# Two rounds of token rows dispatched at once, in float32r products of a high and a low part

## The chip, the cores and the metric

The kernel runs on one core of a Trainium2 chip. Its time is device microseconds of one execution. The core's engines run side by side, each with its own stream of instructions: TensorE (PE) for products, VectorE (DVE), ScalarE (ACT), GpSimd (POOL) and SyncE (SP), which here issues the transfers. Weights come from HBM; tiles lie in SBUF (128 partitions), products go to PSUM.

## The reference

256 tokens of width 1024 pass through a block with a mixer, a cross attention and an expert layer, and then through further stages of the same kind; the kernel meets three expert layers in all. An expert layer computes, for 16 experts in 4 groups:

```
gidx  = best of 4 groups;  eidx = best 2 of the 4 experts in it;  ew = softmax(2 values) * gval
combine[t, e] = weight of expert e for token t, 0 for the 14 others
for e in 16 experts:
    he = silu(t @ w_gate[e]) * (t @ w_up[e])
    y += combine[:, e] * (he @ w_down[e])
```

Each token uses two experts, so the kernel brings tokens to the experts that want them instead of computing all pairs. `w_gate` and `w_up` are 1024x512, `w_down` 512x1024, in float32.

## The kernel before

An expert layer is the function `moe`. First comes the routing: ACT and DVE normalise the rows of the tokens into `xs` (two tiles of 128 tokens x 1024), the logits are formed, and a chain of small DVE operations and an exponential on ACT (L941) picks the experts; products with a triangular matrix (L1053) count each token's place among those of its expert, and `pm` (L1055) holds it. `places` (L1184) then builds one-hots `O`: for two rounds at a time, O[token, slot] is 1 where the token stands in that slot. A round is 128 slots, cut among two to four experts by `ROUNDS`; there are seven rounds (p = 0 to 6).

For each round TensorE does in order:

- `pg` and `pu`: the gate and the up product of the round's 128 slots (`times`, `prod`, L1078), over eight row blocks of the weights.
- `pP`: transposes of the round's one-hots (`back`, L1098), used later to bring results back.
- `px`: the *dispatch* of the next round (L1066): the rows of the tokens are brought to the slots as 8 blocks of xs^T O, each summed over two token tiles. In float32 each product of 128x128 is two instructions, so that a dispatch is 32 of them, in two halves of 16. DVE multiplies the result by the column scale into `XT` (L1068), POOL adds the shift where there is one (L1070).
- `hid`: DVE multiplies silu(pg) by pu (L1090), then `ph` transposes it on TensorE (L1092), and ACT copies it back (L1093). The first half of the next dispatch stands ahead of ph, the second half behind.
- `py`: the down product (L1078 again), then `pc` (L1128, L1129) adds the weighted results to the tokens' rows `x`.

The weight of each slot comes from `slot_weights`, every second round: products `pw` of the one-hots with the experts' weights (L1212), and small DVE reductions `ws` (L1217). The first round's dispatch is `first_inputs` (L1197), evacuated by ACT (L1199, L1201).

The weights are streamed by `Stream.load` (L125) in units of 1 MiB in the fixed order of a plan, into a ring of 20 units; a unit's slot is refilled when its products are done. A tile scheduler sets the order of the instructions on each engine from the order of the code and the buffers; instructions inside `pin` keep their order in the program. `warm` issues filling products on TensorE. After round 3, `extras` is a branch for experts that have more tokens than slots; it isn't entered here.

Of the kernel before, what the change touches and what calls it, by code (L numbers as in the profile page):

```python
# [44 lines left out]
NP8, NP4, NP2 = 22, 2, 7  # L46
# [165 lines left out]
class Kernel:  # L212
# [774 lines left out]
    def moe(self, sx, sc_v, sh_v, first, x, units, ahead=None, start=None, hook=None, st=None, tail=0):  # L987
# [41 lines left out]
        xs = self.b8("xs")  # L1029
        if first:  # L1030
            pin(nc.scalar.activation(xs[:, D:], x[:, D:], AF.Copy, scale=rs[:, 1:2]))
            pin(nc.vector.tensor_scalar(xs[:, :D], x[:, :D], rs[:, 0:1], None, ALU.mult))
        else:
            pin(nc.scalar.activation(xs[:, D:], x[:, D:], AF.Identity, bias=off[:, 1], scale=rs[:, 1:2]))
            pin(nc.vector.tensor_scalar(xs[:, :D], x[:, :D], mu[:, 0], rs[:, 0:1], ALU.subtract, ALU.mult))
# [12 lines left out]
        S.moes += 1  # L1048
        pp = self.aux("pos")
# [10 lines left out]
        def dispatch(O, xt):  # L1060

            for k0 in range(0, 8, 4):
                ps = self.aux("px")
                for c in range(4):
                    for t in range(2):
                        nc.tensor.matmul(ps[:, c * P : (c + 1) * P], xs[:, t * D + (k0 + c) * P : t * D + (k0 + c + 1) * P], O[:, t * P : (t + 1) * P].bitcast(F32), start=(t == 0), stop=(t == 1))  # L1066
                xo = xt[:, k0 : k0 + 4, :]
                nc.vector.tensor_mul(xo, ps[:].rearrange("p (c s) -> p c s", c=4), sc_v[:, k0 : k0 + 4].unsqueeze(2).to_broadcast([P, 4, P]))  # L1068
                if sh_v is not None:
                    nc.gpsimd.tensor_add(xo, xo, sh_v[:, k0 : k0 + 4].unsqueeze(2).to_broadcast([P, 4, P]))  # L1070
                yield
# [8 lines left out]
        def times(xt, get, ps, r):  # L1080
            for kh in range(2):
                ws = get()
                for c in range(4):
                    k = kh * 4 + c
                    prod(ps[:], xt[:, k, :], ws, c, k == 0, k == 7, r)
                del ws
# [84 lines left out]

        def places(p, pm):


            O, out, n0 = self.b2("O", F32R), [], slots(p)[0][0]
            for r in range(p, min(p + 2, len(ROUNDS))):
                o = O[:, (r - p) * 256 : (r - p) * 256 + 256]
                out.append(o)
                o = o.rearrange("p (t s) -> p t s", t=2)
                for w in sorted(set(ROUNDS[r])):  # L1180
                    same = [(s - n0, c) for s, c in slots(r) if CAPS[s] == w]
                    s0, c0, n = *same[0], len(same)
                    sh = [P, 2, n, w]
                    nc.vector.tensor_tensor(  # L1184
                        o[:, :, c0 : c0 + n * w].rearrange("p t (e s) -> p t e s", e=n),
                        pm[:, :, s0 : s0 + n].unsqueeze(3).to_broadcast(sh),
                        self.cst(C_IOTA, w).unsqueeze(1).unsqueeze(1).to_broadcast(sh), ALU.is_equal)
            return out

        def first_inputs(O):  # L1190
            xt = self.b4("XT", F32, (P, 8, P))
            for k in range(8):
                if k % 2 == 0:
                    ps = (self.mm if k > 2 else self.aux)("px")
                q = ps[:, k % 2 * P : k % 2 * P + P]
                for t in range(2):
                    nc.tensor.matmul(q, xs[:, t * D + k * P : t * D + (k + 1) * P], O[:, t * P : (t + 1) * P].bitcast(F32), start=(t == 0), stop=(t == 1))  # L1197
                if sh_v is None:
                    nc.scalar.activation(xt[:, k, :], q, AF.Copy, scale=sc_v[:, k : k + 1])  # L1199
                else:  # L1200
                    nc.scalar.activation(xt[:, k, :], q, AF.Identity, bias=sh_v[:, k : k + 1], scale=sc_v[:, k : k + 1])  # L1201
            return xt

        def inputs(O):
            xt = self.b4("XT", F32, (P, 8, P))
            return xt, dispatch(O, xt)
# [16 lines left out]
        xt = first_inputs(Os[0])  # L1223
# [69 lines left out]
        def prepare(px, pw):  # L1293
# [5 lines left out]
            for k in range(8):  # L1299
                q = px[:, k * 32 : (k + 1) * 32]  # L1300
                for t in range(2):
                    ww = slice(t * D + k * P, t * D + (k + 1) * P)
                    nc.tensor.matmul(q, xs[:, ww], O[:, t, 0, :].bitcast(F32), start=(t == 0), stop=(t == 1))
# [89 lines left out]
        for p in range(LAST + 1):  # L1393
            n = len(ROUNDS[p])
            get, downs = (lambda: [S.raw() for _ in range(n)]), (lambda: [S.raw(down=True) for _ in range(n)])
            if p % 2 == 0:
                wsl = slot_weights(p, Os)
            PT = Os.pop(0)
# [9 lines left out]
            if p == 0 and start is not None:  # L1408
                start(xs)
# [3 lines left out]
            del xt  # L1413
            back(PT, self.aux("pP"))
            if p % 2 and p < LAST:
                s0 = slots(p + 1)[0][0]
                Os = places(p + 1, pm[:, :, s0:])
            if p < LAST:
                xt, fill = inputs(Os[0])
                next(fill)  # L1420
# [3 lines left out]
            if p == LAST:  # L1424
                del xs
# [646 lines left out]
```

## Time and profile before

| | us |
|---|---|
| median of 3 runs | 1337.19 (1334.74 to 1338.62) |
| the profiled execution | 1337.22 |
| its span | 1335.5 |
| TensorE busy | 1248.1 (93%) |
| DVE busy | 714.1 (53%) |
| ACT busy | 405.2 (30%) |
| POOL busy | 127.9 (10%) |
| mean granted TensorE clock | 0.974 of full speed |

The busy shares are averages over stages of different kinds. The expert layers are where transfers run near 420 GB/s for 200 us at a time and DVE is busy for only two or three tenths; between them DVE and ACT are busier and the transfers slower. What a change in one stage is worth is to be read from that stage's own timeline.

### The profile page before, as it was taken

Reading aid. Unit: us, or ns where it says so; the run is one execution under the profiler, and the core shown is the slowest. Engines: PE = TensorE matmul, PEld = TensorE weight load, DVE = VectorE, ACT = ScalarE, POOL = GpSimd, SP = SyncE. Lnnn points to the kernel's source line nnn. Section 1 sums busy time; section 2 is a strip of 40 time slices with the busy share of each in tenths; the row PEclk is TensorE's granted clock in tenths of the full one; section 3 lists DMA queues with packets and bytes.
Section 4 is the critical chain, followed back from the end, with each engine's and each line's share of the span. In section 5 each row is a group of like instructions: output and inputs, shape, how many; then the busy total and the mean of one; then the engine's idle time right before and its main releaser. Section 6 shows DMA issues by size and latency. Waiting matters only on the chain. (4 is left out here: it accounts for less than half of the span.)

```text
span 1335.5 us, 18792 instructions
## 1 busy us (share of the span) xinstructions
PE 1248.1 (93%) x7149; PEld 786.4 (59%) x7149; DVE 714.1 (53%) x1422; ACT 405.2 (30%) x687; POOL 127.9 (10%) x136
## 2 busy tenths in 40 slices
PE   6999988999979989999999979989999999997995
PEld 5677867744334459977543334388988874433442
DVE  5797996532212149875732212388999754222224
ACT  4576434310000034654311000243345541000011
POOL 1000200000000020232010001031102000001001
PEclk9899998899999999999999989999999999998998
DMA  9857795779999997688599999977788578999990
GB/s 375 324 189 266 276 373 225 281 306 421 421 418 422 418 420 273 225 317 314 195 394 421 421 417 421 419 297 267 270 313 318 189 315 323 423 420 419 420 390 31
DMA packets 64509, 445.75 MB, mean 334 GB/s; under 512 B 7380, under 2 KB 7892, under 8 KB 12048
## 3 DMA queue, kind: packets, MB, share of 16 engines
q1 hardware_dynamic: 62352, 439.91, 82.9%
q10 hardware_dynamic: 1440, 3.13, 0.6%
q8 instruction: 61, 1.00, 0.3%
q0 software_dynamic: 608, 1.32, 0.3%
q14 instruction: 48, 0.39, 0.1%
HBM read 443.28 MB, written 1.05 MB: 333 GB/s over the span
## 5 line engine op out<-in xcount | busy, mean ns | idle before, releaser
L173 DVE TENSOR_TENSOR hl<-w,hl 128x1024 fp32r<-128x1024 f32 (+1 forms) x154 | 190.9, 1249 | 51.2 <-ACT hl L172 50.9
L172 ACT CAST hl<-w 128x1024 fp32r<-128x1024 f32 (+1 forms) x160 | 164.9, 1040 | 175.8 <-PE dn L426 107.4
L1078 PE MATMUL pg<-w,XT 128*64 128x512 f32 (+1 forms) x864 | 179.1, 613 | 0.0
L1078 PE MATMUL pu<-w,XT 128*64 128x512 f32 (+1 forms) x864 | 162.2, 593 | 0.0
L1078 PE MATMUL py<-w,hid 128*64 128x512 f32 (+2 forms) x912 | 155.7, 573 | 2.0 <-ACT hid L1093 2.0
L812 DVE SCALAR_TENSOR_TENSOR acc<-w,sc,acc 128x512 f32<-128x512 f32 x168 | 130.2, 779 | 1.6
L1090 DVE TENSOR_TENSOR hid<-hid,pu 128x512 f32<-128x512 f32 x21 | 14.4, 687 | 207.2 <-PE pu L1078 195.7
L1078 PEld LDWEIGHTS pu<-w,XT 128*64 128x64 f32 (+1 forms) x864 | 49.9, 125 | 95.6 <-issue 92.9
L1078 PEld LDWEIGHTS pg<-w,XT 128*64 128x64 f32 (+1 forms) x864 | 49.0, 128 | 96.8 <-issue 94.1
L1078 PEld LDWEIGHTS py<-w,hid 128*64 128x64 f32 (+1 forms) x912 | 48.8, 125 | 90.7 <-issue 81.2
L1401 ACT ACTIVATE hid<-pg 128x512 f32<-128x512 f32 x21 | 12.5, 597 | 209.8 <-PE pg L1078 209.8
L1131 DVE TENSOR_TENSOR x<-x,pc 128x512 f32<-128x512 f32 (+1 forms) x90 | 54.9, 647 | 32.8 <-PE pc L1129 32.2
L1066 PE MATMUL px<-O,xs 128*128 128x128 f32 x576 | 70.8, 276 | 0.0
L1066 PEld LDWEIGHTS px<-O,xs 128*128 128x128 f32 x576 | 67.2, 192 | 3.4 <-issue 3.4
L1117 DVE SCALAR_TENSOR_TENSOR y<-py,ws,gate 128x512 f32<-128x512 f32 x26 | 19.5, 751 | 66.0 <-PE py L1078 66.0
L1070 POOL TENSOR_TENSOR XT<-XT,adaT 128x512 f32<-128x512 f32 x24 | 25.0, 1042 | 299.0 <-DVE XT L1068 289.2
L424 PE MATMUL dn<-hl,h 128*128 128x512 f32 (+1 forms) x128 | 50.8, 403 | 2.9 <-ACT hl L172 2.9
L1118 ACT CAST yh<-y 128x512 fp32r<-128x512 f32 x26 | 16.1, 619 | 120.8 <-DVE y L1117 120.8
L425 PE MATMUL dn<-hl,h 128*128 128x512 f32 (+1 forms) x128 | 51.3, 401 | 0.8 <-DVE hl L173 0.8
L424 PE MATMUL dn<-hl,e 128*128 128x512 f32 x128 | 51.2, 400 | 0.0
L426 PE MATMUL dn<-hl,h 128*128 128x512 f32 (+1 forms) x128 | 51.0, 398 | 0.0
L426 PE MATMUL dn<-hl,e 128*128 128x512 f32 x128 | 49.9, 390 | 0.0
(547 smaller groups left out, 2261.1 us busy)
## 6 DMA issues: line engine op xcount, KB each, us to landing
w<-e SPq DMA_DIRECT2D x282, 1024.0 KB, 14.3
w<-w SPq DMA_DIRECT2D x78, 1024.0 KB, 7.6
w<-wa SPq DMA_DIRECT2D x48, 1024.0 KB, 6.8
w<-e SPq DMA_DIRECT2D x12, 512.0 KB, 16.8
xT<-xT SPq DMA_DIRECT2D x2, 512.0 KB, 5.1
w<-w SPq DMA_DIRECT2D x4, 256.0 KB, 7.0
x<-x SPq DMA_DIRECT2D x2, 512.0 KB, 11.3
mem<-mem SPq DMA_DIRECT2D x2, 512.0 KB, 3.9
```

The source lines that it names most:

```text
L172: a = k.nc.scalar.copy(hi, w)
L173: b = eng.tensor_sub(lo, w, hi.bitcast(F32))
L424: nc.tensor.matmul(o, a, wh[:, c, :], start=(first and c == 0), stop=False)
L425: nc.tensor.matmul(o, a, wl[:, c, :], start=False, stop=False)
L426: nc.tensor.matmul(o, b, wh[:, c, :], start=False, stop=(last and c == m - 1))
L812: pin(nc.vector.scalar_tensor_tensor(acc[:], w[:, j, :], c, acc[:], ALU.mult, ALU.add))
L1066: nc.tensor.matmul(ps[:, c * P : (c + 1) * P], xs[:, t * D + (k0 + c) * P : t * D + (k0 + c + 1) * P], O[:, t * P : (t + 1) * P].bitcast(F ...
L1070: nc.gpsimd.tensor_add(xo, xo, sh_v[:, k0 : k0 + 4].unsqueeze(2).to_broadcast([P, 4, P]))
L1078: nc.tensor.matmul(out[a : a + w, :], lhs[:, a : a + w], ws[e][(slice(None), c, *h)], start=start, stop=stop, tile_position=(0, a))
L1117: nc.vector.scalar_tensor_tensor(y, py, w, gate[:, n * 512 : n * 512 + 512], ALU.mult, ALU.mult)
L1118: nc.scalar.copy(yh, y)
L1131: nc.vector.tensor_add(a, a, pc)
```

## The change

The normalised rows are kept as two float32r tiles instead of one float32 tile: `xh`, the rows rounded by a cast on ACT, and `xl`, the rest, a subtraction on DVE (`low`). In the second and third expert layers the rows are normalised in place in `x` first. A dispatch then serves the two rounds whose one-hots lie in one tile: for each of 8 blocks, four float32r products (xh and xl, two token tiles) with a moving operand of 256 columns, which are the two rounds' one-hots. It runs at the start (for rounds 0 and 1) and in rounds 1, 3 and 5 (for 2 and 3, 4 and 5, and for 6 alone, with the operand repeated). Results of 128x256 are scaled and shifted in one instruction, by ACT and DVE in turn; `first_inputs` and POOL's additions are gone. `slot_weights` is moved behind the up product. Two pools of tiles are larger by one, and the scratch for DMA descriptors is set to 4096.

```
-NP8, NP4, NP2 = 22, 2, 7
+NP8, NP4, NP2 = 23, 3, 7
...
-        xs = self.b8("xs")
+        xh, xl = self.b8("xh", F32R), self.b8("xl", F32R)
         if first:
-            pin(nc.scalar.activation(xs[:, D:], x[:, D:], AF.Copy, scale=rs[:, 1:2]))
-            pin(nc.vector.tensor_scalar(xs[:, :D], x[:, :D], rs[:, 0:1], None, ALU.mult))
+            for t in range(2):
+                pin(nc.scalar.activation(xh[:, t * D : (t + 1) * D], x[:, t * D : (t + 1) * D], AF.Copy, scale=rs[:, t : t + 1]))
         else:
-            pin(nc.scalar.activation(xs[:, D:], x[:, D:], AF.Identity, bias=off[:, 1], scale=rs[:, 1:2]))
-            pin(nc.vector.tensor_scalar(xs[:, :D], x[:, :D], mu[:, 0], rs[:, 0:1], ALU.subtract, ALU.mult))
+            pin(nc.scalar.activation(x[:, D:], x[:, D:], AF.Identity, bias=off[:, 1], scale=rs[:, 1:2]))
+            pin(nc.vector.tensor_scalar(x[:, :D], x[:, :D], mu[:, 0], rs[:, 0:1], ALU.subtract, ALU.mult))
+            for t in range(2):
+                pin(nc.scalar.copy(xh[:, t * D : (t + 1) * D], x[:, t * D : (t + 1) * D]))
+
+        def low(t, lo, hi):
+            c = slice(t * D + lo, t * D + hi)
+            if first:
+                pin(nc.vector.scalar_tensor_tensor(xl[:, c], x[:, c], rs[:, t : t + 1], xh[:, c].bitcast(F32), ALU.mult, ALU.subtract))
+            else:
+                pin(nc.vector.tensor_sub(xl[:, c], x[:, c], xh[:, c].bitcast(F32)))
...
         S.moes += 1
+        low(0, 0, D)
+        low(1, 0, 512)
...
-        def dispatch(O, xt):
+        def dispatch(Os, xt):
...
+            O = [o.rearrange("p (t s) -> p t s", t=2) for o in Os]
+            for k in range(8):
+                if k % 2 == 0:
+                    ps = self.aux("px")
+                q = ps[:, k % 2 * 256 : k % 2 * 256 + 256]
+                for t in range(2):
+                    ww = slice(t * D + k * P, t * D + (k + 1) * P)
+                    o = both[:, :, t, :] if len(Os) == 2 else O[0][:, t].unsqueeze(1).to_broadcast([P, 2, P])
+                    for i, part in enumerate((xh, xl)):
+                        nc.tensor.matmul(q, part[:, ww], o, start=(t == i == 0), stop=(t == i == 1))
+                y = xt[k // 4][:, k % 4, :]
+                if k % 2:
+                    nc.vector.tensor_scalar(y, q, sc_v[:, k : k + 1], 0.0 if sh_v is None else sh_v[:, k : k + 1], ALU.mult, ALU.add)
+                elif sh_v is None:
+                    nc.scalar.activation(y, q, AF.Copy, scale=sc_v[:, k : k + 1])
+                else:
+                    nc.scalar.activation(y, q, AF.Identity, bias=sh_v[:, k : k + 1], scale=sc_v[:, k : k + 1])
+                if k % 4 == 3:
+                    yield
...
         Os = places(0, pm0[:, :, 0::4])
         self.warm(WARM_INPUTS[S.moes - 1])
-        xt = first_inputs(Os[0])
+        low(1, 512, D)
+        xt, fill = inputs(Os)
+        self.do(fill)
...
-            if p % 2 == 0:
-                wsl = slot_weights(p, Os)
-            PT = Os.pop(0)
...
             times(xt, get, pu, p)
-            del xt
+            if p % 2 == 0:
+                wsl = slot_weights(p, Os)
+            PT = Os.pop(0)
             back(PT, self.aux("pP"))
+            fill = ()
             if p % 2 and p < LAST:
+                del xt
                 s0 = slots(p + 1)[0][0]
                 Os = places(p + 1, pm[:, :, s0:])
-            if p < LAST:
-                xt, fill = inputs(Os[0])
+                xt, fill = inputs(Os)
                 next(fill)
             hidden(hid, pu, self.aux("ph"))
             self.do(fill)
...
-    nc = bacc.Bacc("TRN2", target_bir_lowering=False, num_devices=1)
+    nc = bacc.Bacc("TRN2", target_bir_lowering=False, num_devices=1, dynamic_dma_scratch_size=4096)
```

Three places show how the instructions move. The first is TensorE at the end of round 0 of the first expert layer, from the last up product to the first down product; before:

```order
L1078 MATMUL pu_2350<-w_250_1797,XT_2231 64x512
L1098 MATMUL pP_2441<-cst,O_2223 128x128 x2
L1066 MATMUL px_2446<-O_2223,xs_2160 128x128 x8
L1092 MATMUL ph_2456<-cst,hid_2351 128x128 x4
L1066 MATMUL px_2463<-O_2223,xs_2160 128x128 x8
L1078 MATMUL py_2473<-w_265_1892,hid_2351 64x512
```

And after, from the same up product:

```order
L1101 MATMUL pu_2361<-w_250_1797,XT_2236 64x512
L1225 MATMUL pw_2453<-cbr_2343,O_2226 128x32 x4
L1121 MATMUL pP_2462<-cst,O_2226 128x128 x2
L1115 MATMUL ph_2466<-cst,hid_2362 128x128 x4
L1101 MATMUL py_2473<-w_265_1892,hid_2362 64x512
```

The products px on both sides of the transposes ph are gone from this round, and the products pw have come to stand behind the up product.

The second is ACT in the routing of the second expert layer; `pr` is the exponential, `gate` a row of the residual gate. Before:

```order
L1025 COPY lpart_6983<-lp_6973 128x256
L1034 ACTIVATE xs_6987<-x_78,off_6968,xn_6941 128x1024
L941 ACTIVATE pr_7016<-pr_7016 128x32
L901 ACTIVATE gate_6993<-gate_6994,cst 128x512
L901 ACTIVATE gate_6993<-gate_7004,cst 128x512
```

And after:

```order
L1026 COPY lpart_7208<-lp_7198 128x256
L1035 ACTIVATE x_78<-x_78,off_7193,xn_7166 128x1024
L1038 CAST xh_7212<-x_78 128x1024 x2
L902 ACTIVATE gate_7221<-gate_7222,cst 128x512
L942 ACTIVATE pr_7244<-pr_7244 128x32
L902 ACTIVATE gate_7221<-gate_7232,cst 128x512
```

Two casts are added ahead of the exponential, and one gate row that stood behind it now stands ahead of it.

The third is DVE in round 0 of the second expert layer, at the hidden product (`hid`); `kk` and `tab` belong to a table for the block that follows. Before:

```order
L1686 TENSOR_SCALAR tab_7239<-tab_7239 128x256
L1678 TENSOR_SCALAR kk_7240<-kk_7240 128x256
L1090 TENSOR_TENSOR hid_7188<-hid_7188,pu_7187 128x512
L1679 TENSOR_SCALAR kk_7240<-kk_7240 128x256
L1682 SCALAR_TENSOR_TENSOR tab_7239<-kk_7240,ang_7236 128x256
```

And after:

```order
L1694 TENSOR_SCALAR kk_7478<-kk_7478 128x256
L1230 TENSOR_REDUCE ws_7562<-pw_7563 64x1
L1695 TENSOR_SCALAR kk_7478<-kk_7478 128x256
L1230 TENSOR_REDUCE ws_7562<-pw_7563 64x1
L1698 SCALAR_TENSOR_TENSOR tab_7477<-kk_7478,ang_7474 128x256
L1230 TENSOR_REDUCE ws_7562<-pw_7563 64x1
L1698 SCALAR_TENSOR_TENSOR tab_7477<-kk_7478,tab_7477 128x256
L1230 TENSOR_REDUCE ws_7562<-pw_7563 64x1
L1698 SCALAR_TENSOR_TENSOR tab_7477<-kk_7478,tab_7477 128x256
L1113 TENSOR_TENSOR hid_7426<-hid_7426,pu_7425 128x512
```

The reductions of pw, which were done long before, now stand ahead of the hidden product, with operations of the table between them.

## Rows read from the trace of the kernel before

**Rows 1.** Windows, first layer: us, busy PE, PEld, DVE, ACT, POOL; PEclk; DMA; GB/s.
```profile
401.00:484.00 83.00, 81.84 (x403) 34.33 (x404) 16.19 (x30) 11.45 (x18) 0.57 (x1) 0.98 1.01 420
```
**Rows 2.** Timeline of TensorE, end of round 0: start, us, engine, line, operation.
```profile
285.21 0.44 PE L1098 MATMUL pP<-cst,O 128*128 128x128 f32 x2
285.48 1.95 PE L1066 MATMUL px<-O,xs 128*128 128x128 f32 x16
287.27 0.60 PE L1092 MATMUL ph<-cst,hid 128*128 128x128 f32 x4
287.71 1.95 PE L1066 MATMUL px<-O,xs 128*128 128x128 f32 x16
289.59 0.65 PE L1078 MATMUL py<-w,hid 128*64 128x512 f32 x2
```
**Rows 3.** Timeline of TensorE, end of round 6 of the first layer.
```profile
474.20 0.44 PE L1098 MATMUL pP<-cst,O 128*128 128x128 f32 x2
475.12 0.66 PE L1092 MATMUL ph<-cst,hid 128*128 128x128 f32 x4 [0.48 <-DVE hid L1090]
476.45 1.08 PE L1078 MATMUL py<-w,hid 128*64 128x512 f32 x4 [0.68 <-ACT hid L1093]
```
**Rows 4.** Timeline of TensorE, slot weights of the third layer's round 0.
```profile
1106.63 0.62 PE L1212 MATMUL pw<-cbr,O 128*128 128x32 f32 x4
```
**Rows 5.** Timeline of TensorE, a run of 128x256 products behind the first layer.
```profile
498.19 0.28 PE L442 MATMUL dt<-b,hl 128*128 128x256 f32 x1
...
499.99 0.28 PE L442 MATMUL dt<-b,hl 128*128 128x256 f32 x1
```
**Rows 6.** Timeline of TensorE, start of the first layer's dispatch and products.
```profile
265.69 3.36 PE L1197 MATMUL px<-O,xs 128*128 128x128 f32 x28
...
270.63 1.94 PE L1078 MATMUL pg<-w,XT 128*64 128x512 f32 x8
```
**Rows 7.** Timeline of all engines, routing and start of the second layer.
```profile
637.13 1.24 ACT L1034 ACTIVATE xs<-x,off,xn 128x1024 f32<-128x1024 f32 x1
...
639.51 0.23 ACT L941 ACTIVATE pr<-pr 128x32 f32<-128x32 f32 x1 [1.14 <-DVE pr L940]
...
639.82 0.69 ACT L901 ACTIVATE gate<-gate,cst 128x512 f32<-128x512 f32 x1
...
642.28 0.26 DVE L928 SCALAR_TENSOR_TENSOR sl<-er,go 128x16 fp32r<-128x16 f32 x2
...
643.65 0.17 DVE L1055 SCALAR_TENSOR_TENSOR pm<-pos,sl 128x32 f32<-128x32 f32 x1
...
644.43 3.06 PE L1197 MATMUL px<-O,xs 128*128 128x128 f32 x24 [0.22 <-DVE O L1184]
...
649.51 2.79 PE L1078 MATMUL pg<-w,XT 128*64 128x512 f32 x12
```
**Rows 8.** Lines by form, casts and subtractions: count, busy us, mean ns, idle before.
```profile
L173 DVE TENSOR_TENSOR hl<-w,hl 128x1024 fp32r<-128x1024 f32 x150 | 188.2, 1264 | 50.7 <-ACT hl L172 50.4
L172 ACT CAST hl<-w 128x1024 fp32r<-128x1024 f32 x156 | 162.4, 1051 | 175.0 <-PE dn L426 107.4 <-PE dt L443 43.9 <-PE cv L426 11.8
```
**Rows 9.** Lines, the reductions of the slot weights.
```profile
L1217 DVE TENSOR_REDUCE ws<-pw 64x1 f32<-64x2 f32 (+2 forms) x48 | 7.5, 157 | 17.8 <-PE pw L1212 17.2
```
**Rows 10.** Timeline of DVE, the table's operation in the second layer's round 0.
```profile
667.86 0.42 DVE L1682 SCALAR_TENSOR_TENSOR tab<-kk,ang 128x256 f32<-128x256 f32 x1
```
**Rows 11.** Source view of line 125, the unit issued at 335.9 us.
```profile
DMA to landing us min/median/max: 16.9/16.9/16.9
```
**Rows 12.** Timeline of TensorE, first product of round 3.
```profile
357.55 0.59 PE L1078 MATMUL pg<-w,XT 128*32 128x512 f32 x1
```
**Rows 13.** Lines, weight loads of the dispatch.
```profile
L1066 PEld LDWEIGHTS px<-O,xs 128*128 128x128 f32 x576 | 67.2, 192 | 3.4 <-issue 3.4
```
**Rows 14.** Timeline of TensorE, its first products behind the first layer.
```profile
492.47 2.84 PE L355 MATMUL b<-cst,x 128*128 128x128 f32 x16 [3.06 <-DVE x L331]
```
**Rows 15.** Windows of TensorE: us, busy, granted clock, DMA share, GB/s.
```profile
494.00:496.00 2.00, 2.00 (x12) 0.50 1.04 434
```

More of the change, by code (lines that the diff above doesn't have):

```diff
@@ L1058, in moe @@
         del pp
-        def dispatch(O, xt):
[L1062 to L1071, printed above, removed]
+        def dispatch(Os, xt):
[18 more added lines that the diff above has]
+                    yield
         def prod(out, lhs, ws, c, start, stop, r, *h):
@@ L1084, in times @@
                     k = kh * 4 + c
-                    prod(ps[:], xt[:, k, :], ws, c, k == 0, k == 7, r)
+                    prod(ps[:], xt[kh][:, c, r % 2 * P : r % 2 * P + P], ws, c, k == 0, k == 7, r)
                 del ws
@@ L1170, in tiles @@
             }
+        both = None
         def places(p, pm):
+            nonlocal both
             O, out, n0 = self.b2("O", F32R), [], slots(p)[0][0]
+            both = O[:].rearrange("p (r t s) -> p r t s", r=2, t=2)
             for r in range(p, min(p + 2, len(ROUNDS))):
@@ L1188, in places, with inputs @@
             return out
[L1190 to L1206, printed above, removed]
+        def inputs(Os):
+            xt = [self.b4("XT", F32, (P, 4, 256)) for _ in range(2)]
+            return xt, dispatch(Os, xt)
         def slot_weights(p, Os):
@@ L1302, in prepare @@
                     ww = slice(t * D + k * P, t * D + (k + 1) * P)
-                    nc.tensor.matmul(q, xs[:, ww], O[:, t, 0, :].bitcast(F32), start=(t == 0), stop=(t == 1))
+                    for i, part in enumerate((xh, xl)):
+                        nc.tensor.matmul(q, part[:, ww], O[:, t, 0, :], start=(t == i == 0), stop=(t == i == 1))
             nc.vector.tensor_mul(xt, px[:, :256].rearrange("p (c s) -> p c s", c=8), sc_v.unsqueeze(2).to_broadcast([P, 8, 32]))
@@ L1408, in moe @@
             if p == 0 and start is not None:
-                start(xs)
+                start(x)
             if p == XP - 1:
@@ L1424, in moe @@
             if p == LAST:
-                del xs
+                del xh, xl, xt
             down(hid, downs, wsl[:, p % 2 : p % 2 + 1], PT, tiles(p == LAST), p, p == LAST)
```

## The prediction

> **What bounds the kernel now.** I read the page's 40 slices first, then the stretches by engine, then TensorE's timeline over the ends of single rounds, then all engines over the starts of the expert stages, and last when weights were issued, landed and were used. The profiled execution took 1337.22 us, 1335.5 of it span; the median of the runs is 1337.19, so the sum below is made against 1337.2 and needs no shift.
>
> Inside an expert stage the reader is to see two limits close together. TensorE is busy 81.84 of the 83 us from 401 to 484, at a granted clock of 0.98, while the DMA engines are busy all the time (share 1.01, 420 GB/s) [rows 1]. So TensorE's instructions, and the waits between them, set the end, as long as weights keep ahead.
>
> At the end of a round with a dispatch, TensorE goes from the transposes pP through 16 products, the four transposes ph, 16 products more, to py: 285.21 to 289.59, 4.38 us. Sixteen of these products fill 1.79 us (285.48 to 287.27), and they also fill the wait for the hidden product (DVE) and its copy (ACT) [rows 2]. In the last round, which dispatches nothing, those two waits stand open (0.48 and 0.68 us) and pP to py takes 474.20 to 476.45, 2.25 us [rows 3]. This pair is the heart of the forecast: a dispatch taken out is worth 4.38 - 2.25 = 2.13 us, not the 3.58 that its products take.
>
> **A round without a dispatch.** In rounds 0, 2 and 4 the dispatch is gone: -2.13 each. The products pw (0.62 us, [rows 4]) move from the middle of the pg products to behind the pu products in rounds 0 and 4, into the wait for the hidden product. There they cost about nothing, since they and the transposes pP (0.27 until the next start, rows 2) together last about as long as pP and the open 0.48 of rows 3: -0.6 more. Rounds 0 and 4 give -2.7 each. In round 2 pw stays inside a run of products; half of its dispatch lies among the pu products, where it fills no wait, so that nearly its full 1.79 goes; behind ph the other half gives way to an open wait, 2.32 us from ph to py in rows 2 against 1.33 in rows 3, -1.0. That is -2.8 at most; I take -2.6. Round 6 had no dispatch and gains only its pw, which is half as long: -0.3.
>
> **A round with a dispatch for two.** Rounds 1, 3 and 5 now have 32 float32r products of 128x256. The nearest rows are the dt products, float32r with 256 columns and a new weight for each: from 498.19 to 499.99 there are 15, 0.12 us each [rows 5]. So 32 take 3.84 us. With pP (0.27) and ph (0.44 from 287.27 to the next start) the way to py is 4.55 us against 4.38: +0.2 each. The bounds of the price: below, the two float32 instructions' own pitch of 1.79/16 = 0.112 (32 of these are 3.58, then +0.0); above, twice 0.12, if the moving operand, which here is two runs of 128 columns that begin 256 columns apart, and not one run of 256, streams at half the pace. I take 0.12, the row with the same count of columns and the same type. In the last dispatch the second run repeats the first; I price it alike. The evacuations change engine (eight of 128x256, half on ACT and half on DVE, for two DVE products and two Pool additions); both engines are idle there, and TensorE writes two of them in 0.96 us. I cost them at nothing but the tail behind the last product, which is hidden in the down products.
>
> Rounds together: -2.7 - 2.6 - 2.7 - 0.3 + 3 x 0.2 = -7.7 us per stage, three times.
>
> **The start of the first expert stage.** Products start at 265.69 and the gate products are in an unbroken run from 270.63 on, two of them (0.44) having come earlier: they stand as if begun at 270.2 [rows 6]. Now all 32 products stand ahead of pg. The low parts (about 0.8 us per 1024, and 1.5 us of them before the one-hots) lie mostly under the wait for the positions' products; I let the dispatch start 0.6 later, at 266.3. 266.3 + 3.84 + 0.35 for the last evacuation = 270.5: +0.3. If none of the low parts were covered it would be +1.9.
>
> **The start of the other two.** Here something is added to the chain that decides. In [rows 7] ACT normalises the second token tile (637.13, 1.24 us), then waits, then does the routing's exponential at 639.51, which waited for DVE. In the changed order two casts of 1024 columns, 1.05 us each [rows 8], and one gate row (0.69) stand ahead of that exponential: 638.37 + 2.10 + 0.69 = 641.16, so it comes 1.65 later. All of DVE's routing is queued behind that exponential, and behind it the positions, the one-hots and the first product. Then the low parts, 1.26 and about 0.69 (half of the subtraction in rows 8 and a fixed part), stand ahead of the one-hots' positions pm. But seven small operations of the routing that stood there now come later: sl at 642.28 to pm at 643.65 was 1.37 and becomes 0.36 + 1.95 = 2.31. First product: 644.43 + 1.65 + 0.94 = 647.0. Pg then stands as if begun at 647.0 + 3.84 + 0.35 = 651.2, against 649.51 - 0.44 = 649.07: +2.1 with rounding down for what overlaps. The bounds: +0.5 if the scheduler's order lets the casts hide under the wait of 1.14 that ended with the exponential, +4 if TensorE's clock falls in its longer wait (below). I take +2.0 for each of the two stages.
>
> **The second stage's round 0.** There DVE also builds a table for the block that follows (tab, 0.42 each, [rows 10]), and before the hidden product it has a wait for pw now: four small reductions of pw (0.16 each, [rows 9]) alternate with table operations, and the hidden product is behind them all. pw can start only when pu has ended. So the hidden product starts at 0.62 + 4 x 0.16 + 3 x 0.42 + 0.2 = 2.7 us after pu's end, instead of at once; TensorE waits: +2.7, which swallows this round's gain. If the pw reductions were through earlier it is 0; if a further table operation slips ahead, +3.2. The first and third stages have the hidden product ahead of the reductions: nothing.
>
> **The limit by weights.** In the first stage the smallest lead that I found is at the start of round 3: a unit issued at 335.9 landed 16.9 us later, at 352.8 [rows 11], and its products started at 357.55 [rows 12]: 4.7 us ahead. The sum asks -2.7 + 0.2 - 2.6 + 0.3 = -4.8 by then. I take 0.4 off the first stage's gain. The third and second stage ask 3.1 and 0.4 by that place, less than this lead; if it were fully gone, each us asked beyond it would be lost.
>
> **Sum.** First stage -7.7 + 0.3 + 0.4 = -7.0; second -7.7 + 2.0 + 2.7 = -3.0; third -7.7 + 2.0 = -5.7. Together -15.7: 1337.2 - 15.7 = 1321.5, and I forecast 1321.
>
> The larger pools and the smaller scratch for DMA descriptors I cost at nothing: the ring's length and the order of the loads stay. Pool loses 24 additions in a time in which nothing waited for it but the next round's input.
>
> **Weight loads, a rule against the change.** Each dt product of rows 5 has its own load of a 128x128 weight, and the dispatch's loads took 192 ns [rows 13]; yet the products follow at 0.12. Loads lie beside products in flight. The Trainium skill, page "TensorE: Matmul & The Clock Gate", Part 3, "What overlaps and what doesn't", says that a weight load overlaps products in flight only where row groups differ; here all are full height. By that rule a dispatch would be 32 x (0.12 + 0.19) = 9.9 us, 6.1 more for each of 12, and the time 1395. The trace's 0.12 and 0.112 contradict it, so it has no chance of its own beyond a part of the third rival's.
>
> **Rivals.**
> 1. TensorE's clock. After a wait of 3.06 us on TensorE [rows 14] the stretch 494 to 496 had a granted clock of 0.50, 1.2 GHz [rows 15]. In the second and third stage TensorE's wait ahead of the first product grows from 0.22 (rows 7) to 2.8, and in the second stage's round 0 by 2.7. If the dispatch behind that wait runs at half the clock it takes 3.84 us more, twice: 1329. For it: the wait is nearly as long as in rows 14. Against it: filling products (the calls of warm) stand just ahead of it. The same page, "HAM oscillation — how this bites in real kernels", says that pauses between bursts send the next burst to the half clock; rows 14 and 15 agree, and by it the time would be this rival's.
> 2. Weights bind for longer than I allow: the DMA share of 1.01 says that nothing can be fetched faster, and each us that TensorE gains shortens the lead. If only half of the rounds' gain survives in all stages (-23.1 / 2 instead of -23.1), the time is 1333. For it: rows 1. Against it: in rows 1 TensorE, not the wait for weights, filled the stretch.
> 3. Slower: the moving operand in two runs streams at half pace. 32 products then take 7.68 us, +3.84 for each of 12 dispatches: +46, 1368. The sum turns at a price of 0.12 + 15.7 / 384 = 0.161 us per product. For it: no row of before shows a moving operand in two runs in float32r. Against it: in no row that I read does an operand's layout change the pace; rows 2 pass 128 columns at a time at nearly the pace of rows 5.
> 4. The even rounds' waits grow more than rows 3 show, or DVE's and ACT's evacuations hold up the hidden product in the odd rounds; with 0.7 us in each of 18 rounds the gain is 3 us: 1334.
> 5. Better: the low parts and casts are covered, and the second stage's round 0 keeps its gain: 1321.5 - 2 x 1.5 - 2.7 = 1316, and to 1313 if the odd rounds cost nothing and the start is shorter.
>
> **Chances.** The forecast, within 4 us of 1321: 0.54. Clock: 0.13. Weights: 0.10. Growing waits: 0.08. Better: 0.08. Half pace or some other price above 0.16: 0.07. What a measurement of this kernel tells from no change is about 0.3%, 4 us. Faster by more than that: forecast, clock, better, and most of weights and of growing waits: 0.84. Within it: 0.07. Slower: 0.09, with half pace and a start that is worse than every bound. The range leaves out the half pace and the best of the better: 1312 to 1335; the forecast's own is 1317 to 1326.
>
> **What would show it.** In the changed profile the two-round products follow each other at 0.12 us; pP to py takes about 2.3 us in even rounds (5 in round 0 of the second stage) and 4.5 in odd ones. The routing's exponential is 1.7 us later behind the casts, the first product of the second stage comes 2.6 later, and its granted clock stays at 1.00. Py of the first stage's round 2 or pg of round 3 waits a little for a DMA. A pitch above 0.16, a clock of 0.5 at the starts, or waits for weights in rounds 4 to 6 would make the prediction wrong.

## The result, and the profile after

The changed kernel takes 1345.36 us (1344.72 to 1348.17) against 1337.63 for the kernel before on the same chip: a ratio of 1.0065, 95% interval 1.0044 to 1.0087. It is slower by 8 us where 16 us of gain were forecast. The profiled execution has a span of 1343.1 us. TensorE does less than before (1248.1 us busy before), and the end comes later all the same:

```profile
span 1343.1 us, 18206 instructions
PE 1238.3 (92%) x6861; PEld 758.4 (56%) x6861; DVE 714.7 (53%) x1442; ACT 422.8 (31%) x716; POOL 102.5 (8%) x112
```

The first place to look at is a round with a dispatch. This is TensorE's timeline at the end of round 1 of the first layer, in the columns of [rows 2]:

```profile
310.02 0.44 PE L1121 MATMUL pP<-cst,O 128*128 128x128 f32 x2
...
310.41 0.28 PE L1085 MATMUL px<-O,xl 128*128 128x256 f32 x1
310.53 0.28 PE L1085 MATMUL px<-O,xh 128*128 128x256 f32 x1
310.65 0.28 PE L1085 MATMUL px<-O,xl 128*128 128x256 f32 x1
...
311.24 0.28 PE L1115 MATMUL ph<-cst,hid 128*128 128x128 f32 x1
311.55 0.39 PE L1085 MATMUL px<-O,xh 128*128 128x256 f32 x1
...
312.61 0.49 PE L1115 MATMUL ph<-cst,hid 128*128 128x128 f32 x3
312.85 0.36 PE L1085 MATMUL px<-O,xh 128*128 128x256 f32 x1
...
313.98 1.07 PE L1101 MATMUL py<-w,hid 128*64 128x512 f32 x2
314.98 0.38 PE L1085 MATMUL px<-O,xh 128*128 128x256 f32 x1
...
316.12 7.08 PE L1101 MATMUL py<-w,hid 128*64 128x512 f32 x30
323.13 0.50 PE L1151 MATMUL pc<-yh,O 128*128 128x512 f32 x1
```

The products do follow at 0.12 us (310.41, 310.53, 310.65). But the 32 are cut into four pieces of eight, and a lone pair of down products (two instructions, as for every float32 product here) stands between the third and the fourth. That pair takes 1.00 us (313.98 to 314.98); in the run behind it 30 take 7.01, 0.47 for two. From pP to pc the round takes 13.11 us, against 11.40 in the same round before (worked out from the same two instructions there). It was to cost 0.2 more and costs 1.7.

Round 0 of the first layer, which has no dispatch, did what was forecast. There, in the columns of [rows 2], the wait behind ph is open as in [rows 3]:

```profile
283.62 0.62 PE L1225 MATMUL pw<-cbr,O 128*128 128x32 f32 x4
284.09 0.44 PE L1121 MATMUL pP<-cst,O 128*128 128x128 f32 x2
284.53 0.66 PE L1115 MATMUL ph<-cst,hid 128*128 128x128 f32 x4
285.86 7.09 PE L1101 MATMUL py<-w,hid 128*64 128x512 f32 x32 [0.68 <-ACT hid L1116]
```

The path is 283.62 to 285.86, 2.24 us with pw in it: 4.38 of [rows 2] less 2.14.

Round 2 did so in the first layer only. From the first pc of round 1 to the first pc of round 2 it is 2.57 us shorter than before there (2.6 forecast), but 0.96 shorter in the second layer and 0.68 in the third. In these two the trace of before has the whole dispatch behind the up products, as in round 0, and none of it among them; and in the changed kernel pw cuts the up products. The second layer's round 2, before and after:

```profile
724.34 0.44 PE L1098 MATMUL pP<-cst,O 128*128 128x128 f32 x2
...
728.71 4.48 PE L1078 MATMUL py<-w,hid 128*32 128x512 f32 x34
```

```profile
724.22 0.62 PE L1225 MATMUL pw<-cbr,O 128*128 128x32 f32 x4
724.77 3.62 PE L1101 MATMUL pu<-w,XT 128*32 128x512 f32 x26
...
730.57 4.48 PE L1101 MATMUL py<-w,hid 128*32 128x512 f32 x34 [0.68 <-ACT hid L1116]
```

In round 0 of the second layer the forecast had a wait of 2.7 for the hidden product. It is there, at the length forecast, and something follows it. TensorE's timeline, and DVE's over the same time:

```profile
664.39 0.62 PE L1225 MATMUL pw<-cbr,O 128*128 128x32 f32 x4
664.86 0.44 PE L1121 MATMUL pP<-cst,O 128*128 128x128 f32 x2
667.99 1.11 PE L1115 MATMUL ph<-cst,hid 128*128 128x128 f32 x4 [2.70 <-DVE hid L1113]
669.78 9.14 PE L1101 MATMUL py<-w,hid 128*64 128x512 f32 x32 [0.68 <-ACT hid L1116]
```

```profile
666.60 0.16 DVE L1230 TENSOR_REDUCE ws<-pw 64x1 f32<-64x2 f32 x1
666.79 0.43 DVE L1698 SCALAR_TENSOR_TENSOR tab<-kk,tab 128x256 f32<-128x256 f32 x1
667.25 0.69 DVE L1113 TENSOR_TENSOR hid<-hid,pu 128x512 f32<-128x512 f32 x1
```

The 32 down products take 9.14 us in place of 7.09, and the four transposes 1.11 in place of 0.66: the granted clock fell to 0.50, the lower of its two levels. Windows of TensorE, in the columns of [rows 15], around the up products of this round and behind the wait:

```profile
656.00:658.00 2.00, 2.00 (x9) 0.72 1.01 426
658.00:660.00 2.00, 2.00 (x8) 0.50 1.04 434
...
668.00:670.00 2.00, 1.32 (x6) 0.50 1.01 430
```

Over the whole kernel, set against the trace of before: 3.3 us were gained ahead of the first layer, where nothing was changed (half-clock stretches that fell otherwise). From the logits to an unbroken run of gate products the three starts lost 2.4, 2.4 and 2.3; in the first, some 1.6 of it goes with such a stretch too, at 257.5 us, ahead of the first dispatch product: that came 2.0 later than before, and 0.3 in e5, e6 and e8, which have no such stretch there. The rounds gave 3.7 in the first layer, and lost 5.6 in the second and 2.4 in the third. The rest is under 1. The rounds were to give 7.7 in each, less 2.7 in the second. Two half-clock stretches among up products, at 656.9 us and in the third layer's round 5 at 1278.1 us, cost 1.7 each (8.78 us for 32 products in place of 7.09); no term of the forecast holds them.

### The profile page after: what moved, and what is told of

Its sections match the earlier page's. It is cut to its first block, busy times and chain, and to the rows that moved or that the text cites. A ratio compares the mean times of both kernels' runs of the same rounds, so it can differ in the third digit from the quotient of the medians.

```text
span 1343.1 us, 18206 instructions
## 1 busy us (share of the span) xinstructions
PE 1238.3 (92%) x6861; PEld 758.4 (56%) x6861; DVE 714.7 (53%) x1442; ACT 422.8 (31%) x716; POOL 102.5 (8%) x112
## 5 line engine op out<-in xcount | busy, mean ns | idle before, releaser
L1101 PE MATMUL py<-w,hid 128*64 128x512 f32 (+2 forms) x912 | 167.3, 578 | 8.1 <-ACT hid L1116 8.1
L1101 PE MATMUL pu<-w,XT 128*64 128x512 f32 (+1 forms) x864 | 168.4, 602 | 0.0
L1085 PE MATMUL px<-O,xh 128*128 128x256 f32 x192 | 52.0, 304 | 4.6 <-DVE O L1211 2.4
L425 PE MATMUL dn<-hl,e 128*128 128x512 f32 x128 | 51.2, 400 | 0.0
L427 PE MATMUL dn<-hl,e 128*128 128x512 f32 x128 | 49.9, 390 | 0.0
L426 PE MATMUL dn<-hl,e 128*128 128x512 f32 x128 | 49.8, 389 | 0.0
L1085 PEld LDWEIGHTS px<-O,xh 128*128 128x128 f32 x192 | 36.1, 188 | 22.7 <-ACT XT L1092 10.9
```

The source lines that it names most:

```text
L425: nc.tensor.matmul(o, a, wh[:, c, :], start=(first and c == 0), stop=False)
L426: nc.tensor.matmul(o, a, wl[:, c, :], start=False, stop=False)
L427: nc.tensor.matmul(o, b, wh[:, c, :], start=False, stop=(last and c == m - 1))
L1085: nc.tensor.matmul(q, part[:, ww], o, start=(t == i == 0), stop=(t == i == 1))
L1101: nc.tensor.matmul(out[a : a + w, :], lhs[:, a : a + w], ws[e][(slice(None), c, *h)], start=start, stop=stop, tile_position=(0, a))
```

## The experiments

The runs were made on several chips, on which the kernel before takes 1335.1 to 1337.6 us, so that a difference of two runs' medians can be 1 or 2 us off; the ratios are taken on one chip each. The theory after the first look was that the cuts themselves are what costs; the rival, that the cuts are the scheduler's way around something worse.

**e1: the same work in one piece.** The order on TensorE was set by hand:

```
-                        nc.tensor.matmul(q, part[:, ww], o, start=(t == i == 0), stop=(t == i == 1))
+                        pin(nc.tensor.matmul(q, part[:, ww], o, start=(t == i == 0), stop=(t == i == 1)))
```

and the same for pP in odd rounds and for the first down or gate product behind a dispatch.

> The changed kernel with the order of TensorE alone set by hand: the transposes pP of the odd rounds behind the last up product, all dispatch products in one run on either side of ph, and the first down (or gate) product behind the last of them. Theory of the cuts: a dispatch that is cut into pieces by products of other shape pays about 1 us at a lone pair of down products and 0.1 to 0.2 at each other join; odd rounds get 1.25 us shorter (round 3 about 2), the starts 0.5: 15 us in all, 1330. Rival, the evacuation of PSUM: the products would only wait for banks instead, and the time stays within 3 us of 1345.

Measured: 1352.02 us, ratio to the kernel before 1.0125 (1.0108 to 1.0142). Slower still. The cuts are gone, the round takes 14.51 us (313.22 to 327.73), and TensorE waits inside the dispatch. The round is what this run shows, not the total: its trace has 17.1 us of half clock from 644.1 on, where the changed kernel's has 10.2 in two pieces, and its rounds 3 and 4 together, where the order of the down products changed too, are 3.4 to 4.4 us shorter in each layer. Its timeline in round 1, and ACT's:

```profile
313.22 0.44 PE L1123 MATMUL pP<-cst,O 128*128 128x128 f32 x2
...
314.76 0.39 PE L1085 MATMUL px<-O,xh 128*128 128x256 f32 x1 [0.62 <-ACT XT L1090]
...
320.04 0.39 PE L1085 MATMUL px<-O,xh 128*128 128x256 f32 x1 [0.56 <-ACT XT L1090]
...
320.71 7.09 PE L1101 MATMUL py<-w,hid 128*64 128x512 f32 x32
```

```profile
314.23 0.47 ACT L1090 ACTIVATE XT<-px,vec 128x256 f32<-128x256 f32 x1 [0.17 <-PE px L1085]
```

Each of these products is the first of the second block in a bank of PSUM, and it starts when ACT has taken the first block out of the same bank (314.23 + 0.47 = 314.70, then 314.76). So the rival named something real: two blocks share a bank, and the first is evacuated ahead of the second one's products. The blocks don't overlap; what they share is the tile px, which fills one bank, and no run tells whether the scheduler guards the tile or the bank. The Trainium skill, page "PSUM — Partial Sum Buffer", "PSUM bank collisions raise a hardware error", says that two engines must not be on one bank, in the same quarter of its partitions, at once even in different columns, and that a guard goes by bank and not by address; the wait in this trace agrees, and no run here tried to do without it.

**e3: the price of a cut by itself**, on the kernel before. The last four products of each dispatch go behind the first down product:

```
                 for c in range(4):
+                    if k0 == 4 and c == 2:
+                        yield
...
+                    if rest and e == 1 and a == o:
+                        for _ in rest:
+                            pass
+                        rest = ()
```

> The kernel before, float32 dispatch and all, with one thing added: in each of the 18 rounds with a dispatch the last four of its products (eight instructions) stand behind the first down product instead of ahead of it, as in the changed kernel. The work is the same. Theory of the cuts: about 1 us each, 1337.6 + 18 = 1355. Rival, that a cut costs nothing by itself: 1338 (within 3 us).

Measured: 1358.57 us, 1.018 (1.0161 to 1.0199): 23 us for 18 cuts, 1.3 each. Round 0, TensorE, to be set beside [rows 2]:

```profile
281.78 0.44 PE L1106 MATMUL pP<-cst,O 128*128 128x128 f32 x2
...
285.27 1.07 PE L1084 MATMUL py<-w,hid 128*64 128x512 f32 x2
286.27 1.16 PE L1068 MATMUL px<-O,xs 128*128 128x128 f32 x8
...
294.37 0.50 PE L1136 MATMUL pc<-yh,O 128*128 128x512 f32 x1
```

The lone pair takes 1.00 here too (285.27 to 286.27), and the round 12.59 instead of 11.39. So a cut does cost, and the first theory is right on its price. It had the cause wrong: where the cuts are taken away and the evacuation is left as it is, as in e1, waits that cost more stand in their place.

**e5: whole banks.** One edit of the changed kernel, with no order set by hand:

```
-                y = xt[k // 4][:, k % 4, :]
                 if k % 2:
-                    nc.vector.tensor_scalar(y, q, sc_v[:, k : k + 1], 0.0 if sh_v is None else sh_v[:, k : k + 1], ALU.mult, ALU.add)
...
+                    for j in (k - 1, k):
+                        y, q = xt[j // 4][:, j % 4, :], ps[:, j % 2 * 256 : j % 2 * 256 + 256]
+                        if j % 2:
+                            nc.vector.tensor_scalar(y, q, sc_v[:, j : j + 1], 0.0 if sh_v is None else sh_v[:, j : j + 1], ALU.mult, ALU.add)
...
```

> The changed kernel with one edit: the two evacuations of a PSUM bank (two blocks of 256 columns) are issued behind the products of both blocks, instead of the first one between them. No order is set by hand. Theory, corrected: the second block of a bank could not start while ACT read the first (0.62 us of waiting each, seen in the run with the order set by hand), and it was to dodge that wait that the scheduler cut the dispatch into four pieces; with whole banks the dispatch is in one run on either side of ph, a round with one costs 0.3 us more than before instead of 1.7 to 3, and a start 0.5 less: 1328, 17 us less than the changed kernel. Rival, that the cuts come from the queue of evacuations on ACT and DVE or from products that are slower than 0.12: no less than 1342.

Measured: 1330.41 us, 0.9960 (0.9946 to 0.9974), 15 us less than the changed kernel and faster than the kernel before. TensorE in round 1:

```profile
309.09 0.44 PE L1123 MATMUL pP<-cst,O 128*128 128x128 f32 x2
...
311.27 0.60 PE L1117 MATMUL ph<-cst,hid 128*128 128x128 f32 x4
311.63 0.37 PE L1085 MATMUL px<-O,xh 128*128 128x256 f32 x1
...
313.71 7.09 PE L1103 MATMUL py<-w,hid 128*64 128x512 f32 x32
320.73 0.50 PE L1153 MATMUL pc<-yh,O 128*128 128x512 f32 x1
```

Sixteen products, ph, sixteen products, py: 4.62 us from pP to py (the forecast said 4.55), and 11.64 to pc, 0.24 more than before (the forecast said 0.2). This is the order that the prediction had priced. The products' groups over the whole kernel tell it in a line each, idle time before them last; first the changed kernel, then e5:

```profile
L1085 PE MATMUL px<-O,xh 128*128 128x256 f32 x192 | 52.0, 304 | 4.6 <-DVE O L1211 2.4 <-ACT XT L1092 1.6 <-ACT XT L1090 0.5
```

```profile
L1085 PE MATMUL px<-O,xh 128*128 128x256 f32 x192 | 52.4, 307 | 2.4 <-DVE O L1213 2.4
```

The waits for ACT's XT are gone. In the changed kernel they were only 2.1 us; the other 13 are not among the idle times of this line. In the two traces the nine rounds with a dispatch, from pc to pc, are together 15.6 us shorter in e5.

e5 also shows the prediction's first rival at work. TensorE's waits ahead of the first dispatch product of the second layer are those of the changed kernel (1.27 and 1.11 us here, 1.28 and 1.11 there), but where the changed kernel kept its clock, in e5 it fell:

```profile
640.00:642.00 2.00, 2.00 (x12) 0.50 0.00 0
```

From the first dispatch product to the gate products it takes 6.69 us there and 5.39 in the third layer, against 3.98 at the full clock in the first layer: 4.1 us in all. So these waits do not settle by themselves whether the clock falls.

**e10: the cause without the change.** The kernel before, whose DVE takes each bank whole, now takes it in two halves:

```
+                for c0 in (0, 2):
+                    for c in (c0, c0 + 1):
...
+                    xo = xt[:, k0 + c0 : k0 + c0 + 2, :]
+                    nc.vector.tensor_mul(xo, ps[:, c0 * P : c0 * P + 256].rearrange("p (c s) -> p c s", c=2), sc_v[:, k0 + c0 : k0 + c0 + 2].unsqueeze(2).to_broadcast([P, 2, P]))
```

> The kernel before, float32 dispatch, with one thing changed: DVE (and POOL) take each bank of the dispatch in two halves of two blocks, the first ahead of the second half's products. Theory of the shared bank: the scheduler then cuts this dispatch too, with a lone down product, without any float32r product or pair of rounds; at 1.2 us for each of 18 rounds 1336 + 21 = 1357. Rival, that the cuts belong to the larger dispatch: 1336 to 1339.

Measured: 1360.16 us, 1.0170 (1.0145 to 1.0194). Only the evacuation was changed, and the scheduler cuts a float32 dispatch for one round in the same way. Round 0:

```profile
285.05 0.44 PE L1099 MATMUL pP<-cst,O 128*128 128x128 f32 x2
...
288.65 1.07 PE L1079 MATMUL py<-w,hid 128*64 128x512 f32 x2
289.66 1.16 PE L1067 MATMUL px<-O,xs 128*128 128x128 f32 x8
```

So the cuts need neither the float32r products nor the pair of rounds.

**e2 and e6: the wait in the second layer.** e6 keeps pw where it is and issues the reductions behind the hidden product; e2 moved both there, and so took the slot weights from one-hots that had been transposed by then, which changes their values and not the work.

```
             hidden(hid, pu, self.aux("ph"))
+            if p % 2 == 0:
+                reduced(p, npw, wsl, pw)
```

> The changed kernel with the slot weights' products and reductions moved once more, behind the hidden product. Theory: in round 0 of the second layer the wait for the hidden product (2.7 us) goes, and with it the half clock that followed (another 2.7), and in round 2 of each layer the products pw no longer cut the up products (1.0 each): 8.4 us, 1337. Rival: the clock falls there for another reason and the wait is DVE's table, not the reductions: 0 to 3 us, 1343 to 1345.

> The changed kernel with only the small reductions of the slot weights moved behind the hidden product on DVE; the products pw stay behind the up products. Theory: round 0 of the second layer loses its wait of 2.7 us and the half clock behind it (2.7): 1340. If the half clock comes from what stands ahead of the wait, only the 2.7 of the wait: 1342.6.

Measured: e2 1339.47 us (1.0034, 1.0016 to 1.0053), e6 1342.64 (1.0046, 1.0031 to 1.0061). In both traces the wait of 2.70 is gone, and with it the half clock behind it: round 0 of the second layer is 5.2 us shorter in e6 (from the start of its pu to the end of its py), as expected. The total moved by 2.7 only, which by itself is the number of e6's rival; in e6's profiled execution a half-clock stretch came at the third layer's start (1097.4, not in the changed kernel's) and took 2.3 of it. The half clock among the up products (656 to 660 above) stayed in both, so it has another cause.

**e8: the casts behind the exponential.**

```
-            for t in range(2):
-                pin(nc.scalar.copy(xh[:, t * D : (t + 1) * D], x[:, t * D : (t + 1) * D]))
...
         S.moes += 1
+        if not first:
+            for t in range(2):
+                pin(nc.scalar.copy(xh[:, t * D : (t + 1) * D], x[:, t * D : (t + 1) * D]))
```

> The changed kernel with only the two casts of the second and third layer moved on ACT from ahead of the routing's exponential to behind it. Theory: the exponential comes 1.2 us earlier in each of the two layers, the first dispatch product as well unless the casts are then late for the low parts: 1343, 2.4 less. If the casts are late: 1345, no change.

Measured: 1340.68 us, 1.0037 (1.0026 to 1.0049), 4.7 less than the changed kernel by the medians and 3.7 by the ratios. ACT in the second layer's routing, in the changed kernel and in e8:

```profile
631.84 1.24 ACT L1035 ACTIVATE x<-x,off,xn 128x1024 f32<-128x1024 f32 x1
632.99 1.98 ACT L1038 CAST xh<-x 128x1024 fp32r<-128x1024 f32 x2
634.87 0.68 ACT L902 ACTIVATE gate<-gate,cst 128x512 f32<-128x512 f32 x1
635.45 0.22 ACT L942 ACTIVATE pr<-pr 128x32 f32<-128x32 f32 x1
```

```profile
630.98 1.24 ACT L1035 ACTIVATE x<-x,off,xn 128x1024 f32<-128x1024 f32 x1
632.69 0.23 ACT L942 ACTIVATE pr<-pr 128x32 f32<-128x32 f32 x1 [0.47 <-DVE pr L941]
```

The exponential starts 1.71 us after the normalisation in place of 3.61. The path from the logits to the first dispatch product is 1.9 shorter in the second layer and 1.3 in the third, 3.2 together where 2.4 were expected; what is left of the difference is within the spread of the medians. In e8's trace the half clock of the second layer's round 0 is one stretch of 3.4 us instead of two of 3.4 and 6.8, which goes the right way; that it follows from the edit was not shown.

**e4, e9, e11 and e12: what adds up.** e4 joined e1, e2 and e8 (with e2's values), with pP kept behind the last up product in every round. e12 is e5, e6 and e8 together. e9 is e12 with pP and pw kept behind the last up product in every round, and with the order of the dispatch products and of the first gate and down products set by hand as in e1. e11 is the kernel before with pP alone kept there:

```
-                nc.tensor.transpose(ps[:, t * P : (t + 1) * P], O[:, t * P : (t + 1) * P].bitcast(F32), self.ident)
+                m = nc.tensor.transpose(ps[:, t * P : (t + 1) * P], O[:, t * P : (t + 1) * P].bitcast(F32), self.ident)
+                if hold:
+                    pin(m)
...
-            back(PT, self.aux("pP"))
+            back(PT, self.aux("pP"), True)
```

> Both of the first two together, pP behind the up products in every round, and the two casts of the second and third layer behind the routing instead of ahead of its exponential (1.2 us at each start). If the terms add: 1345.4 - 15 - 8.4 - 2.4 = 1319.6, faster than the kernel before by 18 us. If the weights bind instead, the gain stops at some 1330.

> The three edits of this call together (whole banks, reductions behind the hidden product, casts behind the exponential), and the transposes pP and products pw kept behind the last up product in every round. If the terms add: 1345.4 - 17 - 5.4 - 2.4 - 3 (no cut of the up products in rounds 2 and 3) = 1317, some 19 us faster than the kernel before, which is what the forecast for the change had said. If the weights bind: 1328.

> The kernel before, with only the transposes pP kept behind the last up product in every round. It tells how much of the last kernel's 1311 has nothing to do with the change: rounds 2 and 3 lose one or two cuts of the up and gate products, about 1 us each, some 4 us over three layers: 1332. If the cuts there are hidden by waits for weights: 1336.

> The changed kernel with whole banks, the reductions behind the hidden product and the casts behind the exponential, but the order of pP and pw left to the scheduler. If the terms add: 1330.4 - 2.7 (reductions, by the run of that edit alone) - 4.7 (casts alone) = 1323, and the 12 us to 1311 are the order of pP and pw, the cuts in rounds 2 and 3. If the terms help one another through the clock (no half clock at the starts and in round 0): 1315.

| | us | ratio to before, 95% interval |
|---|---|---|
| e4 (order set by hand, half banks) | 1340.54 | 1.0055 (1.0032 to 1.0078) |
| e12 (whole banks, reductions, casts) | 1319.41 | 0.9875 (0.9858 to 0.9891) |
| e11 (before, pP kept back) | 1328.21 | 0.9942 (0.9925 to 0.9958) |
| e9 (e12, order set by hand) | 1310.94 | 0.9810 (0.9797 to 0.9823) |

e4 was to take 1319.6 and failed as e1 did: its round 1 is as long as e1's in each layer. e12 is 26 us below the changed kernel, more than the 22.4 that its three edits gave one by one. e11 says that 8 us were to be had without the change, by not letting pP cut the products of rounds 2 and 3. e9 is 17 us faster than that. In its trace round 2 of the second and third layer is 2.39 us shorter than before, where the changed kernel gave 0.96 and 0.68. And in e9 the weights begin to bind, in the first layer's round 3, where the prediction had seen the shortest lead. The longest of TensorE's waits from 340 to 382 us (us in total, times, longest):

```profile
PE pu L1104 <- DMA w<-e: 2.4, 2, 1.3
```

The same view of the changed kernel and of e12 has no wait for a DMA.

## Why the prediction was wrong

The step that failed is the one that priced the evacuations: "I cost them at nothing but the tail behind the last product". The engines were idle, and it counted their time and not what they hold: a bank that two blocks share is closed to TensorE while one of them is read, by 0.56 to 0.62 us a time in e1. The sign of it stands in the order of the changed kernel's instructions, a lone down product between pieces of the dispatch; the step took the 32 products as a count and not as a place.

- Rounds with a dispatch: +0.2 forecast; +1.7 measured in rounds 1 and 5 (3.9 in the third layer's round 5, with the half clock), and in round 3 +1.75, +2.83 and +2.83. With whole banks +0.24 in round 1, and -0.30, +0.66 and +0.65 in round 3. In the two traces these nine rounds account for 15.6 us between the changed kernel and e5, whose medians differ by 15; the starts differ both ways, as e5 has no cut there but loses 4.1 us to the clock at two of them.
- The price of a product, 0.12, was right, and with it the whole third rival fell: two runs of 128 columns stream as one of 256. Weight loads of 188 ns lay beside the products, as the traces of before had shown.
- Rounds without a dispatch: in round 0, -2.14 and pw's own time, as forecast. Round 2 was forecast at -2.6 in each layer from the first layer's row alone; in the other two it gave 0.96 and 0.68, 3.6 us too little together, and no more than 0.66 with whole banks.
- The second layer's round 0: the wait was forecast at 2.7 and is 2.70. The half clock behind it (2.5 more, from the two rows with 9.14 and 1.11) was in the first rival at the starts; the place was named there ("and in the second stage's round 0 by 2.7"), its price was not put on it. At the second and third start in the profile of the changed kernel the clock stayed at 1.00; in e5's it did not.
- The starts: +2.0 forecast for the second and third layer, +2.4 and +2.3 measured. Two errors nearly cancel there: the second layer's first dispatch product came 2.1 us later and not 2.6, and with the cut it is 4.93 us from there to the gate products (counted as in [rows 6], as if begun without a break), for 4.19 forecast and 3.98 in the first layer of e5. The first start was to lose 0.3 and lost 2.4, 1.6 of it by the half clock ahead of its dispatch.
- The weights did not bind in the changed kernel, which never came as far ahead; they begin to in e9.

Taken together, the terms for the work were right but for round 2, and the forecast of 1321 lies close to what e12 measures (1319.41) once the bank, the reductions and the casts are out of the way. But e12 lacks costs that the forecast had counted (2.7 for the reductions and 3.2 of the casts), and has others that it had not, so that this is not the same sum and the agreement is chance.

Left open: why the clock fell among the up products at 656.9 us in the changed kernel, and at like places in e2, e5 and e6, and not in e9, e11 and e12. Products with weights of four rows stand ahead of it in all of them. They also stand ahead of the up products in the third layer's round 5, where the clock fell in the changed kernel and in e4, e5, e6, e8, e9, e10 and e12, and not in the kernel before, e1, e2, e3 and e11.

## What to carry to other kernels

Price an evacuation by the bank that it closes: when two results share a bank, take both out behind the last product into it, or give each its own bank. Read the order of the new program for lone products of another shape before counting products: a pair cut out of a run cost 1.2 us here, shows as no idle time, and can stand in the place of a wait that would cost more. Setting the order by hand without removing that wait made the round longer (e1, 14.51 us in place of 13.11). And read a round in each layer before taking one layer's row for all: round 2 was not the same in the second and third.

## What the runs showed of the hardware

- A float32r product of 128x256 whose moving operand is two runs of 128 columns takes 0.12 us, as one run does.
- Two down products of 64 columns alone between products of full width take 1.00 us; in a run two take 0.47. That holds beside float32 (e3, e10) and float32r products.
- A wait of 2.70 us on TensorE was followed by the half clock (0.50) for over 5 us of work, 2.5 us of loss; without the wait (e6) there was none at that place.
- After the same two waits ahead of a dispatch (1.28 and 1.11 us; 1.27 and 1.11) the granted clock stayed at 1.00 in the changed kernel and fell to 0.50 in e5, where 32 products and their last evacuation then took 6.69 us in place of 3.98.
